# One matmul of 512 columns for the high and low parts of 256 tokens, with the two halves summed at evacuation

## The chip, the cores and the metric

The kernel runs on one core of a Trainium2 chip. The metric is the time of the program on the device in microseconds (us). The core's engines work in parallel, each through its own list of instructions in order, and wait for each other by semaphores: TensorE (PE, matmuls and their weight loads), VectorE (DVE), ScalarE (ACT), GpSimd (POOL), and SyncE (SP), whose queue starts the loads from DRAM.

## The reference

Two layers of a trunk over 256 latent tokens and 256 context tokens of 1024 features. Each layer is FFN 1, a mixing part (attention, spatial gating, short convolution) and FFN 2. What matters here is an FFN:

```python
def ffn_half_step(h, shift, scale, gate, g, w_in, w_out):
    a, b = jnp.split(modulate(rms_norm(h, g), shift, scale) @ w_in, 2, axis=-1)
    return h + FFN_RESIDUAL_WEIGHT * gate * ((jax.nn.silu(a) * b) @ w_out)
```

w_in is 1024 x 5632, w_out 2816 x 1024. The result is the latent stream alone, so the very last FFN (layer 1, FFN 2) works on 256 tokens; the other three work on all 512.

## The kernel before

Everything is feature-major: 128 features on the partitions, tokens along the columns. To keep float32 accuracy, every operand of a product is split into a high and a low part, and a product of two blocks is three matmuls (mm3, lines 383 to 386): high weights with high x, high weights with low x, low weights with high x, all summed in one PSUM bank. x lies in two tiles xh and xl, the gated activations in gh and gl.

The class Weights streams the weights in order of use: SP loads a raw block of 128 x 1024 (at most 6 ahead, RAWB), ScalarE rounds it to the high part whi (line 125), and VectorE or GpSimd subtracts to get the low part wlo (line 126). At most 5 such pairs (SUBB) exist; W.done(i) frees one, and the preparation of the weight five places on is written into the engines' lists at that place. With W.low = "a" the low parts go to VectorE and GpSimd in turn, with "g" all to GpSimd.

The FFN of 256 tokens (function ffn with ntok = 256, so both is False) goes so. first_one does pair 0 of the input blocks feature by feature, while the norm of x is still being finished; its evacuation, and then the preparation of four weights on GpSimd, follow. Then for each pair m = 1 to 21: pair_a multiplies the a block (8 features x 3 matmuls of 256 columns, half_mm), pair_b the b block, and evac forms silu(a) * b and splits it into gh and gl. The order around one pair in the lists of ScalarE and VectorE is: preparation after the a block (its wlo on GpSimd), preparation after the b block (its wlo on VectorE), evacuation. Then 8 output blocks (out_part, three weights each, 22 features of the gated activations x 3 matmuls) and for each of them the residual (resid), which adds to h and sends the block out. Six PSUM banks (mm_bank) turn over. The evacuation is:

```python
            ACT.activation(sa[:, 0:n], ba[:, 0:n], AF.Silu)
            DVE.tensor_tensor(sa[:, 0:n], sa[:, 0:n], bb[:, 0:n], ALU.mult)
            ACT.activation(st["gh"][:, m, 0:n], sa[:, 0:n], AF.Copy)
            DVE.tensor_tensor(st["gl"][:, m, 0:n], sa[:, 0:n], st["gh"][:, m, 0:n].bitcast(F32), ALU.subtract)
```

The order of every engine's list is that in which the code is written; no scheduler moves anything.

Of the kernel before, what the change touches and what calls it, by code (L numbers as in the profile page):

```python
# [39 lines left out]
# packed per-partition parameters: name -> columns for one layer  # L40
# [20 lines left out]
class Weights:  # L61
    """Streams weights in order: DRAM -> raw tile -> (high, low) float32r parts, ahead of their use.
    SPARE in the stream is room of one weight, left to other uses between its take and its done."""
# [29 lines left out]
    def pump(self, preps=None):  # L93
        """Start the loads that have room, and prepare the parts (at most preps, when held back)."""
# [80 lines left out]
def hybrid_trunk_kernel(ctx: ExitStack, tc: tile.TileContext, io: dict, out: bass.AP):  # L175
# [46 lines left out]
    def new_scratch():  # L222
        """4 KB that hold either sums of the adaLN products or the pieces of a norm"""
        t = tp.tile([128, 4, 256], F32, tag="scratch", name="scratch", bufs=1)
        st["scr"], st["scr_u"], st["scr_d"] = t, 0, 0
        return t
# [14 lines left out]
    # ---------------------------------------------------------------- weight specs  # L241
# [16 lines left out]
    # ---------------------------------------------------------------- adaLN  # L258
    pend = []

    def ada_tile(l, c, t):
        """Products of 2 x 128 rows and 512 columns of one chunk, summed over row blocks on VectorE."""
        half, part = divmod(t, 4)

        def fn(W):
            r, raw = W.take_raw()
            if part == 0:
                st["ada"] = new_scratch()
            acc = st["ada"][:, :, :].rearrange("p (s q) n -> p s (q n)", s=2)
            for kk in range(2):  # L270
                k = 2 * part + kk
                src = raw[:, 512 * kk:512 * kk + 512]
                for s in range(2):
                    cv = cs[:, k, s:s + 1]
                    if k == 0:
                        DVE.tensor_scalar(acc[:, s], src, cv, None, ALU.mult)  # L276
                    else:
                        DVE.scalar_tensor_tensor(acc[:, s], src, cv, acc[:, s], ALU.mult, ALU.add)  # L278
            W.done_raw(r)
            if part == 3:  # L280
                a = st["ada"]
                pend.append([2, lambda: ada_sum(l, c, half, a)])
        return fn
# [38 lines left out]
    # ---------------------------------------------------------------- norms over features  # L322
    def stats(acc, sl, n):
        """diagonals of the rstd of each token of sl, from squares summed over blocks in acc."""
        fin = stats_a(acc, sl, n)
        return fin()
# [25 lines left out]
    def split_norm(src, dst_h, dst_l, rb, a, b=None, eng=None):  # L352
        """high and low parts of src * a * rb (+ b); returns the emission of the low part."""
# [9 lines left out]
    st["xh"] = xp.tile([128, DK, NTOK], F32R, name="xh")  # L363
    st["xl"] = xp.tile([128, DK, NTOK], F32R, name="xl")
# [6 lines left out]
    def staggered(makers):  # L371
        """runs emissions that return a follow-up, each follow-up one later"""
# [14 lines left out]

    def mm3x(bank, xh, xl, wh, wl, first, last):
# [4 lines left out]
    # ---------------------------------------------------------------- residual update  # L393
    def resid(l, gc, j, bank, half, first, last_use=False):
        """h += gate * bank, and its squares into the accumulator of the next norm."""
# [4 lines left out]
        if last_use:  # L400
            return
# [11 lines left out]
    # A norm chain for the halves of the stream, cut in steps that are emitted between other work.  # L413
    def chain(l, i, half):
        """generator: each next() emits one step; the steps use PE, ACT and DVE."""
# [17 lines left out]
    # ---------------------------------------------------------------- FFN  # L433
    def ffn(l, which, ntok, tail, first=None):
        """tail(part): called by the last block to start the chain of what follows."""
# [7 lines left out]
        def half_mm(bank, sub, sl):  # L443
            _, wh, wl = sub
            for k in range(DK):
                mm3(bank[:, sl], wh[:, 128 * k:128 * k + 128], wl[:, 128 * k:128 * k + 128],
                    st["xh"][:, k, sl], st["xl"][:, k, sl], k == 0, k == DK - 1)

        def evac(m, ba, bb):
            n = ntok  # L450
            sa = temp(512, "sa", 2)
            ACT.activation(sa[:, 0:n], ba[:, 0:n], AF.Silu)
            DVE.tensor_tensor(sa[:, 0:n], sa[:, 0:n], bb[:, 0:n], ALU.mult)  # L453
# [3 lines left out]
        def start(W):  # L457
            st["gpool"] = ExitStack()
            gp = st["gpool"].enter_context(tc.tile_pool(name=f"g{l}{which}", bufs=1))
            st["gh"] = gp.tile([128, NPAIR, ntok], F32R, name="gh")  # L460
            st["gl"] = gp.tile([128, NPAIR, ntok], F32R, name="gl")
        job(start)

        def first_two(W):
            """Blocks 0 and 1: the latent half while the norm of the context half is under way."""
# [38 lines left out]
        def first_one(W):  # L504
# [6 lines left out]
            for k in range(DK):  # L511
                step(c)
                for bank, (_, wh, wl) in ((ba, a0), (bb, b0)):
                    mm3(bank[:, sl], wh[:, 128 * k:128 * k + 128], wl[:, 128 * k:128 * k + 128],
                        st["xh"][:, k, sl], st["xl"][:, k, sl], k == 0, k == DK - 1)
# [40 lines left out]
        def out_mm(bank, sub, k0, nk, sl, dst=None):  # L556
            _, wh, wl = sub
            dst = sl if dst is None else dst
            for kk in range(nk):
                k = k0 + kk  # L560
                mm3(bank[:, dst], wh[:, 128 * kk:128 * kk + 128], wl[:, 128 * kk:128 * kk + 128],
# [51 lines left out]
    def boundary(l, i):  # L613
        """tail of the last block before norm i of layer l: work(0..2) is the ctx half in three parts."""
# [18 lines left out]
    # ---------------------------------------------------------------- mixing  # L633
    def mixing(l):
# [35 lines left out]
        def tok_part(banks, subs, k0, n, tiles, W=None):  # L670
            """banks[t] += x[:, tile t] of the rows in subs; frees the weights when W is given"""
# [41 lines left out]
        def lat_tr(names, nk, dh, dl, gain):  # L713
            """transposed normalised latents, times their gains, into dh/dl"""
# [16 lines left out]
        # kv latents  # L731
# [49 lines left out]
        def k_prep(W):  # L781
            """shared rope part of the keys: squares, gains, rotation"""
            kpe = P["kpe"]
            # rope tables with the heads' gains
# [66 lines left out]
        # short gated conv, feature-major; blocks c, x, b per 128 channels  # L851
# [38 lines left out]
        # spatial gating: weights loaded whole, transposed by the host  # L890
# [30 lines left out]
        def y_sg(W):  # L921
            """transposed gated features into y blocks 4, 5"""
# [25 lines left out]
        # up-projections, token-major  # L948
# [110 lines left out]
        # attention  # L1059
# [9 lines left out]
        def A(n):  # L1069
            """transposed queries and keys of a head; returns the emissions of the high and the low parts"""  # L1070
# [22 lines left out]
        def B(n, lows):  # L1093
            """scores and their exponentials; lows are emissions of other work, after the maxima"""
# [52 lines left out]
        def C(n):  # L1147
            """transposed probabilities; returns the emissions of their evacuation"""
# [23 lines left out]
        def Dv(j, s, bk):  # L1172
            """probabilities times values of heads 2j and 2j+1, side by side on the array, for one half of the
            queries; returns the emissions of the evacuation and of the squares"""
# [73 lines left out]
        # output projection  # L1248
# [84 lines left out]
    # ---------------------------------------------------------------- program  # L1333
# [50 lines left out]
    def first_blocks(in_spec, evac, half_mm):  # L1384
        """Blocks 0 to 2 of the first FFN: feature by feature, as the modulation of each becomes known."""
# [103 lines left out]
    # order of the weight stream: the adaLN tiles, which wait for their use in place, come a little later  # L1489
# [29 lines left out]
def _layout(i):  # L1519
# [4 lines left out]
    def cols(v):  # L1524
        """[L, n*128] -> [128, L, n]"""
# [3 lines left out]
    def blocks(w, n):  # L1529
        """[L, K*128, N] -> [L, N/n, 128, K, n]"""  # L1530
# [3 lines left out]
    def flat(w):  # L1534
        """[L, K*128, N] -> [L, 128, K*N]"""
# [77 lines left out]
```

## Time and profile before

| | us |
|---|---|
| median of 3 runs | 1778.43 (1777.52 to 1781.66) |
| span of the profiled execution, first to last instruction | 1778.8 |
| TensorE busy in it | 1715.4 (96%) |
| VectorE, ScalarE, GpSimd busy | 1077.7 (61%), 661.1 (37%), 328.9 (18%) |
| mean granted TensorE clock | 0.983 |

The profile gives the span for the profiled execution and no other time of its own. Busy times of TensorE are modelled ends of pipelined matmuls, so rates are read from the distance of starts. A granted clock of 1.00 is 2.4 GHz, 0.50 is 1.2 GHz.

### The profile page before, as it was taken

The page shows a single profiled execution, that of the slowest core. Times are in us where ns is not written, and L with a number is a line of the kernel's source. Part 1 is how long each engine was busy: PE and PEld are TensorE (multiplying, and loading weights), DVE is VectorE, ACT ScalarE, POOL GpSimd, SP SyncE. Part 2 cuts the span into 40 slices and gives each one's busy share as a digit, 9 for nine tenths or more (in the row PEclk, how much of TensorE's full clock was granted, in tenths as well). Part 3 has the DMA queues.
Part 4 walks back from the last instruction along what each step waited for, and adds up shares of the span by engine and source line. Part 5 has one row for each costly group of instructions (what it writes and reads, how often), then busy time and mean ns, then how long its engine had stood idle before and what let it go on. Part 6 is the DMA issues. An engine that isn't in the chain of part 4 may idle for free.

```text
span 1778.8 us, 24162 instructions
## 1 busy us (share of the span) xinstructions
PE 1715.4 (96%) x9422; PEld 1450.0 (82%) x9422; DVE 1077.7 (61%) x1778; ACT 661.1 (37%) x1124; POOL 328.9 (18%) x210
## 2 busy tenths in 40 slices
PE   8999999999998999999999999999999987889999
PEld 6888888889876688888888888888888986589999
DVE  5667777635578475575766356576765577554332
ACT  4422223224457443222232242222222355554442
POOL 0000000004346522000000030000000165465442
PEclk9999999999999999999999999999999998899999
DMA  8545555523211124454555234454454242136553
GB/s 318 189 158 181 184 182 191 178 84 98 82 60 48 37 70 151 134 176 155 165 175 166 98 107 158 162 164 161 158 174 123 70 142 69 36 116 210 185 180 94
DMA packets 71395, 248.59 MB, mean 140 GB/s; under 512 B 8048, under 2 KB 9584, under 8 KB 71280
## 3 DMA queue, kind: packets, MB, share of 16 engines
q1 hardware_dynamic: 71136, 246.97, 42.3%
q8 instruction: 74, 1.21, 0.3%
q14 instruction: 41, 0.34, 0.1%
q10 hardware_dynamic: 144, 0.07, 0.0%
HBM read 245.96 MB, written 1.05 MB: 139 GB/s over the span
## 4 chain that ended last, share of the span: by engine, by line
PE 87%; DVE 7%; ACT 3%; issue 2%; POOL 1%; DMA 1%; ACTq 0%; POOLq 0%; DVEq 0%
PE mm L384 26%; PE mm L385 25%; PE mm L386 25%; PE mm L389 2%; PE mm L391 2%; PE mm L390 2%; PE sm L288 1%; ACT p L1130 1%; PE sm L1181 1%; DVE mx L1119 1%; PE mm L1363 1%; DMA raw<-in_w_ada 1%; DVE xl L361 1%; PE sm L1076 1%; PE mm L1158 1%
## 5 line engine op out<-in xcount | busy, mean ns | idle before, releaser
L384 PE MATMUL mm<-xh,whi 128*128 128x512 f32 (+1 forms) x1712 | 612.0, 358 | 6.5 <-DVE kvl L723 3.1
L385 PE MATMUL mm<-xl,whi 128*128 128x512 f32 (+1 forms) x1712 | 605.7, 354 | 4.0 <-DVE xl L361 3.4
L386 PE MATMUL mm<-xh,wlo 128*128 128x512 f32 (+1 forms) x1712 | 604.1, 353 | 1.8 <-POOL wlo L126 1.3
L125 ACT ACTIVATE whi<-raw 128x1024 fp32r<-128x1024 f32 (+1 forms) x334 | 339.1, 1020 | 486.3 <-PE mm L385 373.6
L126 POOL TENSOR_TENSOR wlo<-raw,whi 128x1024 fp32r<-128x1024 f32 (+3 forms) x112 | 258.1, 2318 | 1335.7 <-ACT whi L125 1320.3
L126 DVE TENSOR_TENSOR wlo<-raw,whi 128x1024 fp32r<-128x1024 f32 (+2 forms) x222 | 265.9, 1199 | 244.8 <-ACT whi L125 244.8
L384 PEld LDWEIGHTS mm<-xh,whi 128*128 128x128 f32 x1712 | 327.4, 191 | 63.9 <-issue 11.8
L385 PEld LDWEIGHTS mm<-xl,whi 128*128 128x128 f32 x1712 | 327.4, 191 | 48.2 <-DVE xl L361 4.5
L386 PEld LDWEIGHTS mm<-xh,wlo 128*128 128x128 f32 x1712 | 327.4, 191 | 45.6 <-POOL wlo L126 1.5
L278 DVE SCALAR_TENSOR_TENSOR scratch<-raw,cs,scratch 128x512 f32<-128x512 f32 x448 | 307.4, 745 | 0.0
L384 PE MATMUL mm<-gh,whi 128*128 128x512 f32 (+1 forms) x770 | 270.2, 351 | 0.0
L386 PE MATMUL mm<-gh,wlo 128*128 128x512 f32 (+1 forms) x770 | 267.1, 347 | 0.0
L385 PE MATMUL mm<-gl,whi 128*128 128x512 f32 (+1 forms) x770 | 267.0, 347 | 0.0
L454 ACT ACTIVATE gh<-sa 128x512 fp32r<-128x512 f32 (+1 forms) x88 | 50.9, 579 | 310.2 <-DVE sa L453 310.2
L384 PEld LDWEIGHTS mm<-gh,whi 128*128 128x128 f32 x770 | 145.8, 189 | 22.3 <-issue 4.9
L386 PEld LDWEIGHTS mm<-gh,wlo 128*128 128x128 f32 x770 | 145.8, 189 | 18.3
L385 PEld LDWEIGHTS mm<-gl,whi 128*128 128x128 f32 x770 | 145.9, 189 | 17.5
L276 DVE TENSOR_SCALAR scratch<-raw,cs 128x512 f32<-128x512 f32 x64 | 28.2, 484 | 148.9 <-PE sm L288 148.9
L455 DVE TENSOR_TENSOR gl<-sa,gh 128x512 fp32r<-128x512 f32 (+1 forms) x88 | 57.7, 656 | 56.8 <-ACT gh L454 56.8
L453 DVE TENSOR_TENSOR sa<-sa,mm 128x512 f32<-128x512 f32 (+1 forms) x88 | 53.9, 613 | 17.7 <-PE mm L386 16.0
L408 DVE TENSOR_TENSOR acc<-acc,sq 128x256 f32<-128x256 f32 x63 | 41.4, 657 | 35.1 <-ACT sq L407 35.1
L360 ACT ACTIVATE xh<-scratch,mods 128x256 fp32r<-128x256 f32 x88 | 42.8, 506 | 52.9 <-DVE scratch L356 52.9
(207 smaller groups left out, 1457.6 us busy)
## 6 DMA issues: line engine op xcount, KB each, us to landing
raw<-in_w_ffn_in SPq DMA_DIRECT2D x176, 512.0 KB, 3.9
raw<-in_w_ada SPq DMA_DIRECT2D x144, 512.0 KB, 4.2
raw<-in_w_ffn_out SPq DMA_DIRECT2D x64, 512.0 KB, 4.4
raw<-in_w_ffn_out SPq DMA_DIRECT2D x32, 384.0 KB, 3.4
raw<-in_w_mo SPq DMA_DIRECT2D x16, 512.0 KB, 3.5
raw<-in_w_cv SPq DMA_DIRECT2D x12, 512.0 KB, 3.7
raw<-in_w_uv SPq DMA_DIRECT2D x8, 512.0 KB, 3.9
raw<-in_w_q SPq DMA_DIRECT2D x8, 384.0 KB, 3.1
```

Source lines behind the costliest of these rows:

```text
L125: nc.scalar.activation(hi[:, a:b], src, AF.Copy)
L126: eng.tensor_tensor(lo[:, a:b], src, hi[:, a:b].bitcast(F32), ALU.subtract)
L278: DVE.scalar_tensor_tensor(acc[:, s], src, cv, acc[:, s], ALU.mult, ALU.add)
L360: ACT.activation(dst_h, u, AF.Identity, bias=b)
L384: PE.matmul(bank, lhsT=wh, rhs=xh, start=first, stop=False)
L385: PE.matmul(bank, lhsT=wh, rhs=xl, start=False, stop=False)
L386: PE.matmul(bank, lhsT=wl, rhs=xh, start=False, stop=last)
L389: PE.matmul(bank, lhsT=xh, rhs=wh, start=first, stop=False)
L408: DVE.tensor_tensor(acc[:, half], acc[:, half], sq, ALU.add)
L453: DVE.tensor_tensor(sa[:, 0:n], sa[:, 0:n], bb[:, 0:n], ALU.mult)
L454: ACT.activation(st["gh"][:, m, 0:n], sa[:, 0:n], AF.Copy)
L455: DVE.tensor_tensor(st["gl"][:, m, 0:n], sa[:, 0:n], st["gh"][:, m, 0:n].bitcast(F32), ALU.subtract)
```

## The change

x2 holds high and low parts of x side by side, [128, 8, 2, 512], and g2 those of the gated activations, [128, 22, 2, tokens]; xh, xl, gh and gl become views of them. In the FFN of 256 tokens mm2 takes the place of mm3: one matmul of 512 columns multiplies the high weights with high and low parts at once, into the two halves of a bank, and one of 256 columns adds low weights times high part to the second half. So an evacuation has to sum the halves: ScalarE copies the first half of each bank to SBUF, VectorE adds the second, and Silu, product and split follow. The residual adds the halves of the output one after the other. The rest of the program keeps its order and its operations. (The lines that only lose comments are left out.)

```diff
+    st["x2"] = xp.tile([128, DK, 2, NTOK], F32R, name="x2")
+    st["xh"] = st["x2"][:, :, 0]
+    st["xl"] = st["x2"][:, :, 1]
...
+    def mm2(bank, wh, wl, x2, first, last):
+        PE.matmul(bank, lhsT=wh, rhs=x2, start=first, stop=False, skip_group_check=True)
+        PE.matmul(bank[:, 256:512], lhsT=wl, rhs=x2[:, 0], start=False, stop=last, skip_group_check=True)
...
         DVE.scalar_tensor_tensor(h[:, j, half], src, mods[:, l, gc, j, s:s + 1], h[:, j, half], ALU.mult, ALU.add)
         if last_use:
+            DVE.scalar_tensor_tensor(h[:, j, half], bank[:, 256:512], mods[:, l, gc, j, s:s + 1], h[:, j, half],
+                                     ALU.mult, ALU.add)
             return
...
             for k in range(DK):
+                if not both:
+                    mm2(bank, wh[:, 128 * k:128 * k + 128], wl[:, 128 * k:128 * k + 128],
+                        st["x2"][:, k, :, sl], k == 0, k == DK - 1)
+                    continue
...
             sa = temp(512, "sa", 2)
-            ACT.activation(sa[:, 0:n], ba[:, 0:n], AF.Silu)
-            DVE.tensor_tensor(sa[:, 0:n], sa[:, 0:n], bb[:, 0:n], ALU.mult)
+            if both:
+                ACT.activation(sa[:, 0:n], ba[:, 0:n], AF.Silu)
+                DVE.tensor_tensor(sa[:, 0:n], sa[:, 0:n], bb[:, 0:n], ALU.mult)
+            else:
+                sb = temp(512, "sa", 2)
+                for part, bk in ((0, ba), (1, bb)):
+                    p = sa[:, 256 * part:256 * part + 256]
+                    ACT.activation(sb[:, 256 * part:256 * part + 256], bk[:, 0:n], AF.Copy)
+                    DVE.tensor_tensor(p, sb[:, 256 * part:256 * part + 256], bk[:, 256:512], ALU.add)
+                ACT.activation(sb[:, 0:n], sa[:, 0:n], AF.Silu)
+                DVE.tensor_tensor(sa[:, 0:n], sb[:, 0:n], sa[:, 256:512], ALU.mult)
             ACT.activation(st["gh"][:, m, 0:n], sa[:, 0:n], AF.Copy)
             DVE.tensor_tensor(st["gl"][:, m, 0:n], sa[:, 0:n], st["gh"][:, m, 0:n].bitcast(F32), ALU.subtract)
...
+            st["g2"] = gp.tile([128, NPAIR, 2, ntok], F32R, name="g2")
+            st["gh"] = st["g2"][:, :, 0]
+            st["gl"] = st["g2"][:, :, 1]
...
                 k = k0 + kk
+                if not both:
+                    mm2(bank, wh[:, 128 * kk:128 * kk + 128], wl[:, 128 * kk:128 * kk + 128],
+                        st["g2"][:, k, :, sl], k == 0, k == NPAIR - 1)
+                    continue
```

first_one calls mm2 in the same way. Two places of the engines' lists show the change. ScalarE, in the input part of this FFN, from the evacuation of one pair to that of the next, before (whi is the high part of a weight, raw the loaded block, mm a PSUM bank, sa the temporary of the evacuation):

```order
L452 ACTIVATE sa<-mm 128x256
L454 ACTIVATE gh<-sa 128x256
L125 ACTIVATE whi<-raw 128x1024 x2
L452 ACTIVATE sa<-mm 128x256
L454 ACTIVATE gh<-sa 128x256
```

The same place with the change (g_12906 is the tile g2):

```order
L473 ACTIVATE sa<-mm 128x256 x2
L475 ACTIVATE sa<-sa 128x256
L477 ACTIVATE g_12906<-sa 128x256
L125 ACTIVATE whi<-raw 128x1024 x2
L473 ACTIVATE sa<-mm 128x256 x2
```

Between the two preparations of one pair and those of the next there are now two copies, Silu and gh in place of Silu and gh. VectorE at the same place, before (wlo is the low part of a weight):

```order
L126 TENSOR_TENSOR wlo<-raw,whi 128x1024
L453 TENSOR_TENSOR sa<-sa,mm 128x256
L455 TENSOR_TENSOR gl<-sa,gh 128x256
L126 TENSOR_TENSOR wlo<-raw,whi 128x1024
L453 TENSOR_TENSOR sa<-sa,mm 128x256
```

And with the change:

```order
L126 TENSOR_TENSOR wlo<-raw,whi 128x1024
L474 TENSOR_TENSOR sa<-sa,mm 128x256 x2
L476 TENSOR_TENSOR sa<-sa 128x256
L478 TENSOR_TENSOR g_12906<-sa,g_12906 128x256
L126 TENSOR_TENSOR wlo<-raw,whi 128x1024
```

Where VectorE had the product alone between its low part and gl, it has two sums with a PSUM operand and then a product of two operands in SBUF.

## Rows read from the trace of the kernel before

**Rows 1.** The page's chain that ended last, share of the span by engine

```profile
PE 87%; DVE 7%; ACT 3%; issue 2%; POOL 1%; DMA 1%; ACTq 0%; POOLq 0%; DVEq 0%
```

**Rows 2.** Window in the last stage: us, busy (instructions) by engine, clock, DMA

```profile
1640.00:1660.00 20.00, 20.00 (x169) 20.00 (x168) 6.37 (x10) 9.18 (x14) 8.76 (x4) 1.00 0.56 192
```

**Rows 3.** Groups by shape, last stage: line, operation, count | busy, mean ns

```profile
L384 PE MATMUL mm<-gh,whi 128*128 128x256 f32 x176 | 49.8, 283 | 0.0
```

**Rows 4.** Timeline of TensorE: 24 starts of 256 columns, 18 of 512

```profile
1649.87 0.28 PE L384 MATMUL mm<-xh,whi 128*128 128x256 f32 x1
...
1652.75 0.28 PE L384 MATMUL mm<-xh,whi 128*128 128x256 f32 x1
...
699.89 0.39 PE L384 MATMUL mm<-xh,whi 128*128 128x512 f32 x1
...
703.97 0.39 PE L384 MATMUL mm<-xh,whi 128*128 128x512 f32 x1
```

**Rows 5.** Timelines of ScalarE, VectorE, GpSimd, one pair [idle before <-releaser]

```profile
1648.56 1.06 ACT L125 ACTIVATE whi<-raw 128x1024 fp32r<-128x1024 f32 x1 [1.71 <-issue]
1649.53 0.37 ACT L452 ACTIVATE sa<-mm 128x256 f32<-128x256 f32 x1
1651.24 0.42 ACT L454 ACTIVATE gh<-sa 128x256 fp32r<-128x256 f32 x1 [1.35 <-DVE sa L453]
1651.57 1.04 ACT L125 ACTIVATE whi<-raw 128x1024 fp32r<-128x1024 f32 x1
1654.32 1.06 ACT L125 ACTIVATE whi<-raw 128x1024 fp32r<-128x1024 f32 x1 [1.71 <-issue]
...
1649.65 1.23 DVE L126 TENSOR_TENSOR wlo<-raw,whi 128x1024 fp32r<-128x1024 f32 x1 [3.30 <-ACT whi L125]
1650.80 0.41 DVE L453 TENSOR_TENSOR sa<-sa,mm 128x256 f32<-128x256 f32 x1
1651.69 0.42 DVE L455 TENSOR_TENSOR gl<-sa,gh 128x256 fp32r<-128x256 f32 x1 [0.48 <-ACT gh L454]
...
1646.92 2.40 POOL L126 TENSOR_TENSOR wlo<-raw,whi 128x1024 fp32r<-128x1024 f32 x1 [3.36 <-ACT whi L125]
```

**Rows 6.** Timeline of GpSimd early in the input part

```profile
1613.22 2.41 POOL L126 TENSOR_TENSOR wlo<-raw,whi 128x1024 fp32r<-128x1024 f32 x1 [2.89 <-ACT whi L125]
1618.52 2.41 POOL L126 TENSOR_TENSOR wlo<-raw,whi 128x1024 fp32r<-128x1024 f32 x1 [2.89 <-ACT whi L125]
```

**Rows 7.** Timelines of GpSimd and VectorE where their operations meet

```profile
1596.13 2.40 POOL L126 TENSOR_TENSOR wlo<-raw,whi 128x1024 fp32r<-128x1024 f32 x1
...
1598.49 3.38 POOL L126 TENSOR_TENSOR wlo<-raw,whi 128x1024 fp32r<-128x1024 f32 x1
...
1597.81 1.80 DVE L126 TENSOR_TENSOR wlo<-raw,whi 128x1024 fp32r<-128x1024 f32 x1 [6.96 <-ACT whi L125]
1599.53 0.41 DVE L453 TENSOR_TENSOR sa<-sa,mm 128x256 f32<-128x256 f32 x1
1600.42 1.73 DVE L455 TENSOR_TENSOR gl<-sa,gh 128x256 fp32r<-128x256 f32 x1 [0.48 <-ACT gh L454]
```

**Rows 8.** Timelines around the first evacuation, and ScalarE at pair 3

```profile
1590.30 4.83 ACT L125 ACTIVATE whi<-raw 128x1024 fp32r<-128x1024 f32 x5
...
1593.85 0.39 PE L386 MATMUL mm<-xh,wlo 128*128 128x256 f32 x1 [1.33 <-POOL wlo L126]
...
1612.10 1.04 ACT L125 ACTIVATE whi<-raw 128x1024 fp32r<-128x1024 f32 x1
```

**Rows 9.** Windows elsewhere in which the granted clock falls

```profile
1024.00:1029.00 5.00, 3.25 (x26) 2.84 (x24) 4.27 (x7) 2.63 (x6) 2.56 (x3) 1.00 0.54 166
1029.00:1033.50 4.50, 4.31 (x23) 4.31 (x24) 4.33 (x10) 1.50 (x4) 2.37 (x1) 0.62 0.31 112
```

**Rows 10.** Timeline at the end: last matmul, last residual

```profile
1775.03 0.28 PE L386 MATMUL mm<-gh,wlo 128*128 128x256 f32 x1
1775.35 0.48 DVE L399 SCALAR_TENSOR_TENSOR h<-mm,mods,h 128x256 f32<-128x256 f32 x1 [7.43 <-PE mm L386]
```

More of the change, by code (lines that the diff above doesn't have):

```diff
@@ L361, in split_norm @@
         return lambda: eng.scalar_tensor_tensor(dst_l, u, b, dst_h.bitcast(F32), ALU.add, ALU.subtract)
-    st["xh"] = xp.tile([128, DK, NTOK], F32R, name="xh")
-    st["xl"] = xp.tile([128, DK, NTOK], F32R, name="xl")
+    st["x2"] = xp.tile([128, DK, 2, NTOK], F32R, name="x2")
+    st["xh"] = st["x2"][:, :, 0]
+    st["xl"] = st["x2"][:, :, 1]
     def mod_chunk(l, i, k, half, rb):
@@ L459, in start @@
             gp = st["gpool"].enter_context(tc.tile_pool(name=f"g{l}{which}", bufs=1))
-            st["gh"] = gp.tile([128, NPAIR, ntok], F32R, name="gh")
-            st["gl"] = gp.tile([128, NPAIR, ntok], F32R, name="gl")
+            st["g2"] = gp.tile([128, NPAIR, 2, ntok], F32R, name="g2")
+            st["gh"] = st["g2"][:, :, 0]
+            st["gl"] = st["g2"][:, :, 1]
         job(start)
@@ L513, in first_one @@
                 for bank, (_, wh, wl) in ((ba, a0), (bb, b0)):
-                    mm3(bank[:, sl], wh[:, 128 * k:128 * k + 128], wl[:, 128 * k:128 * k + 128],
-                        st["xh"][:, k, sl], st["xl"][:, k, sl], k == 0, k == DK - 1)
+                    mm2(bank, wh[:, 128 * k:128 * k + 128], wl[:, 128 * k:128 * k + 128],
+                        st["x2"][:, k, :, sl], k == 0, k == DK - 1)
             finish(c)
```

## Prediction

> **What bounds the kernel now.** I read first the chain of work that ended last: TensorE holds 87% of it [rows 1]. The change touches only the last stage, the second FFN of layer 1, which works on the 256 latent tokens (22 pairs of input blocks, then 8 output blocks). So I read that stage by itself: in a window in its middle TensorE is busy all 20 us at a granted clock of 1.00, the 2.4 GHz level [rows 2]. In the output part alone there are 176 instructions for each of the three products [rows 3]; with 44 × 8 triples of the input part the stage has 352 + 176 = 528 triples.
>
> Next the price of a matmul. 24 starts of 256 columns take 2.88 us, 120.0 ns each; 18 starts of 512 columns take 4.08 us, 226.7 ns each [rows 4]. At 2.4 GHz the columns alone would be 106.7 and 213.3 ns, so either width carries the same 13.3 ns on top.
>
> Then the other engines, because a TensorE that is always busy hides how near they are. One pair is one period: ScalarE's whi starts at 1648.56 and again at 1654.32, so 5.76 us, which is 48 matmuls of 120 ns [rows 5]. Inside it the engines hand each other one chain: GpSimd's wlo (1646.92, 2.40 us, so until 1649.32), VectorE's wlo on the whi of 1648.56 (1649.65), the product of the gate (1650.80), gh on ScalarE (1651.24), then the second whi of the pair (1651.57), on which the next wlo of GpSimd waits; one period after 1646.92 that is 1652.68, 1.11 us behind the whi. Two facts about that chain decide this case.
>
> First, VectorE's wlo starts only 0.33 us after GpSimd's wlo ended [rows 5], and when they meet, one waits for the other. At 1597.81 VectorE's wlo was issued while GpSimd's ran (1596.13 + 2.40 = 1598.53); it took 1.80 us where it takes 1.23 us alone, and ended 1.08 us after GpSimd did. GpSimd's next one, begun at 1598.49, took 3.38 us where 2.40 is its own. gl at 1600.42 took 1.73 us instead of 0.42 and ended at 1602.15, 0.28 us after that GpSimd operation (1601.87). The product L453 at 1599.53, which reads one operand from PSUM, took its 0.41 us beside the same GpSimd operation [rows 5, 7]. So operations with both inputs in SBUF are locked out, those with one in PSUM are not. The Trainium skill, page "SBUF", section "Who interferes with whom", says just this (two SBUF inputs on VectorE contend with a GpSimd instruction that reads SBUF, and the later one fully blocks); the rows agree, and of this change the rule says that a slower evacuation can collide.
>
> Second, where the chain is closed by this lock it has a length of its own: second whi to GpSimd 1.11, GpSimd 2.40, end of VectorE's wlo 1.08 later, then product (starting 0.08 before that end, 0.41), gh (0.03 later), next whi (0.33 later): 5.28 us. The trace shows the chain running so: after the stage's slow start GpSimd's wlos start at 1613.22 and 1618.52, 5.30 us apart [rows 6], catching up on TensorE until its 5.76 us rule again. The slack of this loop is thus 0.46 us a pair.
>
> **The change part by part.**
> TensorE: of each triple the two products with the high weights become one instruction of 512 columns. One start fewer per triple: 226.7 + 120.0 = 346.7 ns instead of 360.0, so 13.3 ns × 528 = 7.0 us over the stage, 16 × 346.7 ns = 5.55 us a pair instead of 5.76. The moving operand now has two pieces of 256, which no row shows; bounds are no cost and 13.3 ns again (nothing gained); I take no cost, since the extra goes by instruction at both widths. The Trainium skill, page "TensorE: Matmul & The Clock Gate", section "Back-to-back issue gap", puts the fixed part at 2.5 ns when warm; by that the stage would gain only 1.3 us. The rows give 13.3 ns at two widths, and I keep those.
>
> Evacuation of a pair: before, Silu from PSUM, product, gh, gl. Now copy a, copy b (ScalarE), sum a, sum b (VectorE), Silu, product, gh, gl. The copies stand behind the first whi and are done while VectorE still works on its wlo, so they cost nothing as long as that wlo covers them (0.7 us for two at 0.37, against 1.23 us or more). After that wlo there was one operation of 0.41 us up to gh. Now there are sum a (0.41, PSUM operand as L453), Silu (from SBUF; between 0.37 as from PSUM and 0.42 as gh; I take 0.42) and the product with both inputs in SBUF (0.42 as gl), with 0.03 us for each of two more handovers: 0.90 us longer. Bounds: 0.82 with the short Silu and one handover less, 1.0 with handovers of 0.06; nothing is excluded, since the three follow from each other. Sum b lies beside Silu.
>
> What that does: the second whi comes 0.9 us later, GpSimd's wlo ends 0.9 us later, and 0.33 us was all the distance that there was to VectorE's wlo. They collide, and the loop closes at 5.30 + 0.90 = 6.20 us a pair. TensorE wants 5.55. Queued behind the blocked wlo are the sums, behind them on ScalarE Silu, gh and both whi: everything that feeds TensorE goes at 6.20. Five prepared weights hide this for some pairs; from then on each pair waits some 0.65 us for a low part.
>
> The sum, in the times of the profiled execution. (1) The first block now waits for the low part of each feature at a still halved clock, and gains a little later: about +0.1. (2) The first evacuation gates five weights: the first whi after it starts at 1590.30, and TensorE goes on at 1593.85, when GpSimd has the low part [rows 8]; the evacuation is 0.9 longer. (3) Three more evacuations until the loop runs free: the second whi of pair 3 stood at 1612.10 [rows 8] and moves by 0.1 + 0.9 + 3 × 0.9, and the product of pair 1 meets a GpSimd operation, which costs about the 1.3 us that gl lost [rows 7]: 5.0 us, so 1617.1. (4) 18 pairs at 6.20: 111.6, so 1728.7 for the place where the next second whi would follow gh of pair 21; its gl ends 0.5 later, 1729.2. (5) TensorE needs that g as block 21 of the first output block and has done all before: it waits there, by about 5 us. From there 1 + 7 × 22 = 155 pairs of matmuls at 346.7 ns: 53.7 us, end near 1783.0. Before, the last matmul started at 1775.03 and its slot ended at 1775.15 [rows 10]: +7.9. (6) The last residual is two operations of 0.48 us, the second waiting for the first: +0.5. (7) A wait of 5 us halves the clock: elsewhere, after 5 us in which TensorE worked 3.25, the next 4.5 us ran at a mean of 0.62 [rows 9], so 3.4 us of them at half, the 1.2 GHz level, which costs up to 1.7; bounds 0 and twice that; I take 1.4. Together +9.8 us. The profiled span of 1778.8 us is 0.4 above the median of 1778.43, so 1788.2 us.
>
> **The rivals.**
> No collision. If VectorE's wlo were not held up (the sum, Silu and product together under 0.33 us, or a blocked wlo that costs nothing), TensorE stays the bound: −7.0, plus 0.9 for the first evacuation, 0.1, 0.5 and 0.3 for triples whose gain falls into waits: −5.2, 1773.2 us. For it speaks that busy shares of ScalarE and VectorE are half empty [rows 2]; against it the 0.33 us and the locked operations in rows 7. Chance 7%.
> Half the length. If the added work took 0.45 us, the loop would be 5.75: 18 × 0.45 = 8.1 us less than in (4), some 1.6 us less in (3), and no wait long enough for (7): −1.3, about 1777 us, no difference. The point where the result turns is about 0.5 us of extra evacuation. Chance 7%.
> No gain per instruction. If the second piece costs 13.3 ns, the loop rules the input part anyway, and the output part loses its 155 × 13.3 ns = 2.1 us: 1790.3 us. Chance 10%, within the slower cases.
>
> **How the numbers follow.** The forecast and its variant with no gain: 86%, slower. Its own range: 18 × ±0.1 us for the loop, ±1.3 for the start, −1.4 to +2 for the clock and 2.1 for the pieces: 1784.5 to 1791.5. For 8 in 10 of all cases I go to 1783.5. A difference of 0.2%, 3.6 us, is about what can be told from none: faster 0.07, same 0.07, slower 0.86.
>
> **What would show it.** After the change: starts of GpSimd's wlo 6.2 us apart in the input part (5.55 would refute the collision); VectorE's wlo near 2.5 us instead of 1.23; from about the middle of the input part on, waits of TensorE for wlo of some 0.65 us once a pair; one wait of about 5 us for gl in the first output block, with a halved clock behind it; matmul starts 226.7 and 120.0 ns apart; two operations of 0.48 us at the end. Wrong would be the forecast if blocked operations overlap after all, or if the preparation runs further ahead than the five weights allow.

## The result, and the profile after

The changed kernel takes 1789.75 us (median of 5 runs, 1788.46 to 1791.44); the kernel before took 1778.43 beside it. The ratio is 1.006, with an interval of 1.0047 to 1.0072: slower by about 11 us. The forecast was 1788.2, and its range of 1783.5 to 1791.5 holds the time.

TensorE's share of the chain that ended last fell; shares of the span by engine, page of the changed kernel:

```profile
PE 79%; DVE 8%; ACT 6%; issue 6%; POOL 1%; DMA 1%; ACTq 0%; POOLq 0%; DVEq 0%
```

It was 87% [rows 1]. What TensorE waits for from 1585 us to the end stands in the view of waits of the changed kernel (engine and line, what it waited for, us in total, times, longest):

```profile
PE mm L394 <- POOL wlo L126: 5.4, 12, 1.9
PE mm L393 <- DVE g L478: 4.5, 1, 4.5
```

Twelve waits are for a low part from GpSimd, and one, of 4.5 us, for the gated activations (g, gl in the kernel before). The first of the twelve, 1.9 us, is the one that the kernel before also had at its first evacuation, there 1.33 us [rows 8]. The loop that makes the other eleven is seen in one pair, in the timelines of ScalarE, VectorE and GpSimd of the changed kernel (start, us, engine, line; in brackets the idle time before and who ended it):

```profile
1588.08 4.83 ACT L125 ACTIVATE whi<-raw 128x1024 fp32r<-128x1024 f32 x5
...
1607.38 1.99 ACT L125 ACTIVATE whi<-raw 128x1024 fp32r<-128x1024 f32 x2
...
1613.57 1.99 ACT L125 ACTIVATE whi<-raw 128x1024 fp32r<-128x1024 f32 x2
...
1644.58 1.99 ACT L125 ACTIVATE whi<-raw 128x1024 fp32r<-128x1024 f32 x2
...
1649.56 0.42 ACT L475 ACTIVATE sa<-sa 128x256 f32<-128x256 f32 x1 [2.44 <-DVE sa L474]
1650.47 0.42 ACT L477 ACTIVATE g<-sa 128x256 fp32r<-128x256 f32 x1 [0.49 <-DVE sa L476]
1650.79 1.99 ACT L125 ACTIVATE whi<-raw 128x1024 fp32r<-128x1024 f32 x2
...
1646.61 2.58 DVE L126 TENSOR_TENSOR wlo<-raw,whi 128x1024 fp32r<-128x1024 f32 x1 [1.47 <-ACT whi L125]
1649.12 0.74 DVE L474 TENSOR_TENSOR sa<-sa,mm 128x256 f32<-128x256 f32 x2
1650.01 0.42 DVE L476 TENSOR_TENSOR sa<-sa 128x256 f32<-128x256 f32 x1 [0.15 <-ACT sa L475]
...
1645.70 2.41 POOL L126 TENSOR_TENSOR wlo<-raw,whi 128x1024 fp32r<-128x1024 f32 x1 [3.80 <-ACT whi L125]
1651.91 2.40 POOL L126 TENSOR_TENSOR wlo<-raw,whi 128x1024 fp32r<-128x1024 f32 x1 [3.80 <-ACT whi L125]
```

Follow it from the whi of 1644.58: GpSimd starts 1.12 us later and runs until 1648.11. VectorE's wlo is issued at 1646.61, while GpSimd runs, and ends at 1649.19, 1.08 us after GpSimd; it takes 2.58 us where it took 1.23 [rows 5]. From its end to the next whi (1650.79) the evacuation takes 1.60 us; before, it was 0.69 us from 1650.88 to 1651.57 [rows 5]. So 1.12 + 2.41 + 1.08 + 1.60 = 6.21 us, which is the distance of the two whi and of GpSimd's two starts, and nothing in this circle waits for TensorE. The hold is what makes the circle long: by an estimate from these rows, a wlo of 1.23 us would have ended at 1647.84, and the circle would be 3.26 + 1.60 = 4.86 us, under the 5.55 that TensorE wants. Two whi now follow each other without a pause (one row x2), where there were 1.71 us of idle time between them [rows 5]. ScalarE stands idle for 2.44 us ahead of its Silu, and the releaser named there, the sum, was itself queued behind the blocked wlo.

What that leaves for TensorE, and the clock behind the long wait, is in the windows of the changed kernel (from:to, us, busy and instructions of PE, PEld, DVE, ACT, POOL, granted clock, DMA share, GB/s):

```profile
1640.00:1660.00 20.00, 19.61 (x112) 16.78 (x110) 13.25 (x16) 10.74 (x21) 8.59 (x4) 1.00 0.50 162
1660.00:1680.00 20.00, 18.87 (x103) 15.45 (x102) 13.66 (x16) 9.83 (x18) 7.69 (x4) 1.00 0.48 159
...
1722.00:1724.00 2.00, 0.00 (x0) 0.00 (x0) 1.94 (x3) 0.35 (x1) 0.20 (x1) 0.88 0.38 61
1724.00:1726.00 2.00, 0.52 (x1) 0.50 (x2) 0.85 (x2) 1.49 (x3) 0.00 (x0) 0.50 0.95 313
1726.00:1728.00 2.00, 2.00 (x8) 1.63 (x6) 0.00 (x0) 1.99 (x4) 0.70 (x1) 0.50 0.39 150
1728.00:1730.00 2.00, 2.00 (x8) 1.71 (x7) 1.80 (x1) 1.11 (x2) 1.94 (x2) 0.50 0.00 0
1730.00:1732.00 2.00, 2.00 (x12) 1.76 (x11) 1.13 (x4) 0.85 (x1) 2.00 (x1) 0.91 0.85 219
```

Around 1650 TensorE is still nearly full, on the weights that were ready; from 1660 on it loses 1.1 us in 20. From 1722 to 1724 no matmul runs, the first after the wait starts at 1725.48, and the granted clock falls to 0.50, the 1.2 GHz level; by the five rows some 6.8 us pass at that level. What a pair of matmuls (512 and 256 columns) takes there is seen in TensorE's timeline of the changed kernel, in which four pairs lie between these two starts:

```profile
1726.29 0.63 PE L393 MATMUL mm<-g,whi 128*128 128x512 f32 x1
...
1728.85 0.63 PE L393 MATMUL mm<-g,whi 128*128 128x512 f32 x1
```

That is 640 ns a pair.

The start and the output part show in TensorE's and VectorE's timelines of the changed kernel:

```profile
1577.81 0.79 PE L393 MATMUL mm<-x,whi 128*128 128x512 f32 x1 [1.64 <-DVE x L361]
...
1585.08 0.39 PE L393 MATMUL mm<-x,whi 128*128 128x512 f32 x1
...
1588.55 0.39 PE L393 MATMUL mm<-x,whi 128*128 128x512 f32 x1
...
1725.48 0.79 PE L393 MATMUL mm<-g,whi 128*128 128x512 f32 x1 [4.51 <-DVE g L478]
...
1744.73 0.40 PE L393 MATMUL mm<-g,whi 128*128 128x512 f32 x1
...
1748.97 0.40 PE L393 MATMUL mm<-g,whi 128*128 128x512 f32 x1
...
1782.18 0.40 PE L393 MATMUL mm<-g,whi 128*128 128x512 f32 x1
...
1782.74 0.48 DVE L407 SCALAR_TENSOR_TENSOR h<-mm,mods,h 128x256 f32<-128x256 f32 x1 [6.77 <-PE mm L394]
1783.26 0.48 DVE L409 SCALAR_TENSOR_TENSOR h<-mm,mods,h 128x256 f32<-128x256 f32 x1
```

From 1585.08 to 1588.55 there are 10 pairs of matmuls, 347 ns each, as forecast; from 1744.73 to 1748.97 there are 12, and they take 353.3 ns each. The last residual stands at 1782.74, and its second half follows at 1783.26, where one operation stood before [rows 10].

**The last FFN by segments.** The stage begins for this count at the load of the Silu table on ScalarE (1578.10 us in the profile before, 1574.13 after) and ends with the last residual. In us:

| segment | before | after | more | forecast |
|---|---|---|---|---|
| table load to TensorE's first matmul | 3.10 | 3.68 | 0.58 | in the next |
| to the first whi behind the first evacuation | 9.10 | 10.27 | 1.17 | 1.0, with the one above |
| to the second whi of pair 3 | 21.80 | 25.49 | 3.69 | 4.0 |
| to the last residual | 163.25 | 169.17 | 5.92 | 4.3 |
| its end | 0.48 | 1.00 | 0.52 | 0.5 |
| sum | 197.73 | 209.61 | 11.88 | 9.8 |

The 11.9 us answer to the 11.3 between the medians. The spans differ by only 7.8 (1786.6 and 1778.8), because the profiled execution before came 4.0 us later to this stage, through parts in which both kernels have the same instructions. So below the stage length of each profiled execution, counted in this way, stands beside the median.

### The profile page after: what moved, and what is told of

Same layout as the page of the kernel before. It is cut to its first block, busy times and chain, and to the rows that moved or that the text cites. A ratio compares the mean times of both kernels' runs of the same rounds, so it can differ in the third digit from the quotient of the medians.

```text
span 1786.6 us, 23263 instructions
## 1 busy us (share of the span) xinstructions
PE 1714.6 (96%) x8894; PEld 1421.1 (80%) x8894; DVE 1123.1 (63%) x1830; ACT 673.3 (38%) x1168; POOL 328.0 (18%) x210
## 4 chain that ended last, share of the span: by engine, by line
PE 79%; DVE 8%; ACT 6%; issue 6%; POOL 1%; DMA 1%; ACTq 0%; POOLq 0%; DVEq 0%
PE mm L386 22%; PE mm L387 22%; PE mm L388 22%; ACT whi L125 3%; PE mm L393 2%; PE mm L399 2%; PE mm L397 2%; PE mm L398 2%; PE mm L394 1%; PE sm L288 1%; ACT p L1158 1%; DVE mx L1147 1%; PE mm L1391 1%; DVE x L361 1%; PE sm L1209 1%
## 5 line engine op out<-in xcount | busy, mean ns | idle before, releaser
L386 PE MATMUL mm<-x,whi 128*128 128x512 f32 (+1 forms) x1360 | 512.0, 376 | 5.5 <-DVE kvl L751 3.1
L387 PE MATMUL mm<-x,whi 128*128 128x512 f32 (+1 forms) x1360 | 505.8, 372 | 4.0 <-DVE x L361 3.4
L388 PE MATMUL mm<-x,wlo 128*128 128x512 f32 (+1 forms) x1360 | 504.3, 371 | 0.5 <-DVE wlo L126 0.5
L386 PEld LDWEIGHTS mm<-x,whi 128*128 128x128 f32 x1360 | 259.5, 191 | 62.2 <-issue 11.8
L387 PEld LDWEIGHTS mm<-x,whi 128*128 128x128 f32 x1360 | 259.6, 191 | 48.6 <-DVE x L361 4.9
L388 PEld LDWEIGHTS mm<-x,wlo 128*128 128x128 f32 x1360 | 259.6, 191 | 44.0 <-DVE wlo L126 0.9
L386 PE MATMUL mm<-g,whi 128*128 128x512 f32 (+1 forms) x594 | 220.4, 371 | 0.0
L388 PE MATMUL mm<-g,wlo 128*128 128x512 f32 (+1 forms) x594 | 217.3, 366 | 0.0
L387 PE MATMUL mm<-g,whi 128*128 128x512 f32 (+1 forms) x594 | 217.2, 366 | 0.0
L386 PEld LDWEIGHTS mm<-g,whi 128*128 128x128 f32 x594 | 112.0, 189 | 22.4 <-issue 4.9
L393 PE MATMUL mm<-x,whi 128*128 128x512 f32 x352 | 127.2, 404 | 1.8 <-DVE x L361 1.6
L388 PEld LDWEIGHTS mm<-g,wlo 128*128 128x128 f32 x594 | 112.0, 189 | 18.4
L387 PEld LDWEIGHTS mm<-g,whi 128*128 128x128 f32 x594 | 112.1, 189 | 17.5
L394 PE MATMUL mm<-x,wlo 128*128 128x256 f32 x352 | 101.1, 287 | 5.1 <-POOL wlo L126 5.1
L393 PEld LDWEIGHTS mm<-x,whi 128*128 128x128 f32 x352 | 67.4, 191 | 18.7 <-DVE x L361 2.4
```

The costliest lines, as they stand in the source:

```text
L386: PE.matmul(bank, lhsT=wh, rhs=xh, start=first, stop=False)
L387: PE.matmul(bank, lhsT=wh, rhs=xl, start=False, stop=False)
L388: PE.matmul(bank, lhsT=wl, rhs=xh, start=False, stop=last)
L393: PE.matmul(bank, lhsT=wh, rhs=x2, start=first, stop=False, skip_group_check=True)
L394: PE.matmul(bank[:, 256:512], lhsT=wl, rhs=x2[:, 0], start=False, stop=last, skip_group_check=True)
```

## The experiments

The theory of the prediction (A in the expectations) is that the longer evacuation closes a loop in which VectorE's low part must wait for GpSimd's. If so, the loop must open when one of its links is taken away, the merged matmul alone must cost nothing, and the evacuation alone must bring the whole loss. The other letters are explained in the expectations where they stand. The kernels ran in two sets, each beside runs of the kernel before, which took 1779.79 in the first (20 runs) and 1779.0 in the second (21 runs).

**1. No low parts on GpSimd from pair 1 on** (set 1). VectorE makes all of them, so it has nobody to wait for; the preparations right behind the first evacuation stay on GpSimd.

```diff
             W.done(b0[0])
-            W.low = "a"
+            W.low = "v"
```

> The changed kernel, but in the last FFN all low parts of weights from pair 1 on are made by VectorE, so GpSimd is out of the loop. Theory A (the loop GpSimd low part, blocked VectorE low part, longer evacuation, next high part paces the input part at 6.20 us a pair): the loop is gone, TensorE paces at 16 times 353 ns = 5.65 us a pair, no wait for gl in the first output block; 11.3 us slower than before turns into about 2 us faster, 1776.5 us. Theory B (the sums and copies themselves, whoever makes the low parts, or the two-piece matmul, hold TensorE back): stays at 1787 to 1791 us. Theory C (VectorE becomes the bound with both low parts): its work in a pair is 2 x 1.23 + 0.74 + 0.42 + 0.42 = 4.0 us, so not expected; it would show VectorE without idle time and more than 1780 us.

1778.58 us (10 runs), ratio to before 0.9989 (0.9978 to 1.0001); stage 197.39 us. Waits, VectorE's timeline and windows of this kernel:

```profile
PE mm L394 <- POOL wlo L126: 1.9, 1, 1.9
```

```profile
1645.39 1.23 DVE L126 TENSOR_TENSOR wlo<-raw,whi 128x1024 fp32r<-128x1024 f32 x1 [0.52 <-ACT whi L125]
```

```profile
1590.00:1592.00 2.00, 2.00 (x9) 1.73 (x8) 1.56 (x1) 0.41 (x1) 2.00 (x2) 0.61 0.71 242
1592.00:1594.00 2.00, 2.00 (x8) 1.69 (x7) 0.49 (x1) 1.00 (x2) 2.00 (x1) 0.54 0.61 205
1640.00:1660.00 20.00, 20.00 (x116) 17.34 (x114) 14.30 (x23) 11.64 (x22) 0.00 (x0) 1.00 0.60 188
```

The evacuation is as long as in the changed kernel, and VectorE has all the low parts to make. Yet its wlo is back at 1.23 us, the wait for g is gone, TensorE is full in the middle, and 11 us of time are back. So it was not the amount of work on VectorE or ScalarE but GpSimd's part in the loop: the hold, or its 2.40 us a low part, which experiment 5 tells apart. Some 2 us under before were expected; the interval doesn't show that this kernel is faster than before. What is left is the wait of 1.9 us at the first evacuation, and in this execution the clock fell behind it as well.

**2. The long evacuation with the old matmuls** (set 1). The kernel before, with copy, VectorE operation with a PSUM operand, Silu and product as in the change; the VectorE operation takes the larger of the copy and the bank, which are the same value.

```diff
...
+                    ACT.activation(sb[:, 256 * part:256 * part + 256], bk[:, 0:n], AF.Copy)
+                    DVE.tensor_tensor(p, sb[:, 256 * part:256 * part + 256], bk[:, 0:n], ALU.max)
+                ACT.activation(sb[:, 0:n], sa[:, 0:n], AF.Silu)
+                DVE.tensor_tensor(sa[:, 0:n], sb[:, 0:n], sa[:, 256:512], ALU.mult)
```

> The kernel before with its three matmuls of 256 columns, but with the evacuation of the last FFN made as long as the changed one: both banks copied to SBUF by ScalarE, VectorE takes the maximum of copy and bank (the same value) where the change adds the halves, then Silu from SBUF and a product of two operands in SBUF. Theory A: the longer evacuation alone closes the loop at 6.20 us a pair although TensorE asks for a pair only every 5.76; some 1790 us, wait of about 4.5 us for gl in the first output block. Theory B' (the matmul of 512 columns in two pieces is what costs): 1778 to 1780 us, starts of GpSimd's low parts 5.76 us apart.

1790.53 us (4 runs), ratio 1.0062 (1.0045 to 1.0079); stage 209.60 us, that of the changed kernel. Waits and GpSimd's timeline of this kernel:

```profile
PE mm L384 <- ACT gh L463: 4.0, 1, 4.0
PE mm L386 <- POOL wlo L126: 3.4, 9, 1.9
```

```profile
1644.54 2.42 POOL L126 TENSOR_TENSOR wlo<-raw,whi 128x1024 fp32r<-128x1024 f32 x1 [3.80 <-ACT whi L125]
1650.76 2.40 POOL L126 TENSOR_TENSOR wlo<-raw,whi 128x1024 fp32r<-128x1024 f32 x1 [3.80 <-ACT whi L125]
```

The same two waits and the same 6.2 us a pair, with not one matmul changed. The evacuation alone costs the whole loss, and the merged matmul gives nothing back that can be told as long as this loop sets the pace.

**3. Edits 1 and 2 together** (set 1): old matmuls, long evacuation, VectorE alone.

> As the run with three matmuls and the long evacuation, but all low parts of the last FFN from pair 1 on on VectorE. Theory A: no collision, TensorE paces at 5.76 us a pair; only the first evacuation is 0.9 us longer: 1779.3 us, no difference that can be told. Theory B (length of the evacuation by itself): as slow as with GpSimd, 1788 to 1791 us.

1780.16 us (10 runs), ratio 1.0007 (0.9996 to 1.0018); stage 199.37 us, and the wait at the first evacuation is the only one from there on. Once its loop is open, the long evacuation costs nothing that the medians can tell; the stage of the profiled execution is 1.6 us longer than before, which is about the first evacuation and the longer wait behind it.

**4. The merged matmul with the old evacuation** (set 1). Silu and product read only the first half of each bank; the sum with the second half is left out.

```diff
...
-                for part, bk in ((0, ba), (1, bb)):
...
+            ACT.activation(sa[:, 0:n], ba[:, 0:n], AF.Silu)
+            DVE.tensor_tensor(sa[:, 0:n], sa[:, 0:n], bb[:, 0:n], ALU.mult)
```

> The changed kernel with the short evacuation of before: Silu and product read the first halves of the banks alone, the second halves (products with low x and low weights) are left out of the input part's result. The matmuls are those of the change, low parts by VectorE and GpSimd in turn. Theory A: the loop stays at 5.3 us, under TensorE's 16 x 353 ns = 5.65 us a pair; the merged matmul alone is worth 528 x 6.7 ns = 3.5 us less 0.5 for the second residual: 1775.5 us. Theory B' (the two-piece matmul costs): 1785 us or more.

1773.46 us (5 runs), ratio 0.9958 (0.9942 to 0.9973): 6.3 us faster, more than was expected. The stage in its profiled execution is 195.38 us, only 2.4 us shorter than before, so for about 4 us of that difference this execution gives no place. GpSimd's timeline of this kernel:

```profile
1642.02 2.41 POOL L126 TENSOR_TENSOR wlo<-raw,whi 128x1024 fp32r<-128x1024 f32 x1 [3.25 <-ACT whi L125]
1647.67 2.41 POOL L126 TENSOR_TENSOR wlo<-raw,whi 128x1024 fp32r<-128x1024 f32 x1 [3.24 <-ACT whi L125]
```

5.65 us a pair are 16 × 353.3 ns: TensorE sets the pace. The loop does not bind: early in the stage, where it catches up, GpSimd's starts are 5.30 us apart here too (1609.18 and 1614.48).

**5. The two engines change places** (set 2). GpSimd makes the low part that stands ahead of the evacuation, VectorE the one behind it; they still take turns.

```diff
-                eng = nc.gpsimd if self.low == "g" or (self.low == "a" and self.prep_i % 2) else nc.vector
+                eng = nc.gpsimd if self.low == "g" or (self.low == "a" and self.prep_i % 2 == 0) else nc.vector
```

> The changed kernel with the two low parts of a pair exchanged: GpSimd makes the one of the weight prepared just ahead of the evacuation, VectorE the one prepared behind it. GpSimd still makes half of them. Theory A (it is the chain second high part, GpSimd, blocked VectorE low part, evacuation that closes): now GpSimd's operation lies beside the copies and sums, which read PSUM and are not held up; only the product waits for its end, some 3.8 us after the first high part starts, the second high part comes at 4.2 and the loop is some 5.2 us, under TensorE's 5.65: no pacing wait, about 1776 to 1779 us. Theory D (any use of GpSimd beside this evacuation holds VectorE up, wherever it lies): 1785 us or more.

1775.07 us (10 runs), ratio 0.9982 (0.9973 to 0.9991); stage 194.08 us. Timelines of GpSimd and VectorE of this kernel:

```profile
1642.14 2.40 POOL L126 TENSOR_TENSOR wlo<-raw,whi 128x1024 fp32r<-128x1024 f32 x1 [3.14 <-ACT whi L125]
1647.69 2.42 POOL L126 TENSOR_TENSOR wlo<-raw,whi 128x1024 fp32r<-128x1024 f32 x1 [3.15 <-ACT whi L125]
...
1642.37 0.75 DVE L474 TENSOR_TENSOR sa<-sa,mm 128x256 f32<-128x256 f32 x2 [0.42 <-ACT sa L473]
1643.28 1.55 DVE L476 TENSOR_TENSOR sa<-sa 128x256 f32<-128x256 f32 x1 [0.16 <-ACT sa L475]
...
1646.26 1.23 DVE L126 TENSOR_TENSOR wlo<-raw,whi 128x1024 fp32r<-128x1024 f32 x1 [0.52 <-ACT whi L125]
```

Here the evacuation itself meets GpSimd (1642.14 to 1644.54). Both sums, with a PSUM operand, go through beside it in 0.75 us; the product, with two operands in SBUF, takes 1.55 us instead of 0.42 and ends at 1644.83, 0.29 us after GpSimd. The Trainium skill, page "SBUF — State Buffer", section "Who interferes with whom", draws the line just there: a VectorE instruction with at most one SBUF input does not contend with GpSimd, one with two SBUF inputs contends with a GpSimd instruction that reads SBUF. The rows agree. One lock a pair is paid, 1.1 us, and still the pace is 5.55 us a pair, TensorE's. So here a lock costs time only where it closes a loop longer than TensorE's period: GpSimd's work now stands beside the sums and not ahead of them. What the expectation calls D has fallen, and so has GpSimd's 2.40 us by themselves as the cause of the loss, since they are still paid once a pair. The median lies 1 us under the range that was expected, with pairs of matmuls at 5.55 / 16 = 0.347 us, where 0.353 had been put.

**6. Edit 1, and the first preparations ahead of the first evacuation** (set 2). In first_one the preparation of two weights, on VectorE, is written ahead of the evacuation that it stood behind.

```diff
             W.hold = False
+            W.low = "v"
+            W.pump(2)
             evac(0, ba, bb)
             W.done(a0[0])
             W.done(b0[0])
-            W.low = "a"
```

> The changed kernel with the low parts of the last FFN on VectorE, and with two weights prepared ahead of the first evacuation instead of behind it. Theory A: besides the loop the wait of 1.9 us behind the first pair is gone too, and with it a halved clock that follows it in some executions; against the run with VectorE alone 2 to 3.5 us less, some 4.5 us below before: 1774.5 us. If that wait was hidden or moves to the next weight: as the run with VectorE alone.

1770.36 us (5 runs), ratio 0.9959 (0.9945 to 0.9972): faster than both kernels, and 4 us under what was expected. The stage takes 189.86 us, and TensorE has no wait in it from 1585 us on. Window and TensorE's timeline of this kernel:

```profile
1640.00:1660.00 20.00, 20.00 (x117) 17.48 (x116) 13.96 (x21) 12.49 (x21) 0.00 (x0) 1.00 0.60 193
```

```profile
1699.88 0.39 PE L393 MATMUL mm<-x,whi 128*128 128x512 f32 x1
...
1705.08 0.40 PE L393 MATMUL mm<-g,whi 128*128 128x512 f32 x1
```

15 pairs in 5.20 us, 346.7 ns each, without a seam from the input part (x) to the output part (g). Against kernel 1 the stage is 7.5 us shorter. 1.9 us are the wait; about 1.7 us the clock (some 3.4 us at half); and some 500 pairs at 346.7 ns instead of the 353.3 that kernel 1 shows are 3.3 us: 6.9 us together.

**7. The kernel before with the two edits of 6** (set 2).

> The kernel before, with its three matmuls and short evacuation, and with the same two edits (low parts on VectorE, two weights prepared ahead of the first evacuation). It tells what of the gain of the other run is the merged matmul's. Its wait behind the first pair was 1.5 us: 1.5 us less than before, 1777.5 us; the merged matmul is then worth the rest, 528 x 6.7 ns = 3.5 us less 0.5 for the second residual. If the merged matmul is worth nothing, both runs are equal.

1778.39 us (11 runs), ratio 0.9997 (0.9987 to 1.0007); stage 196.22 us, no wait either from 1585 us on. The edits alone bring the old kernel nothing that the medians can tell (its wait behind the first pair, which the expectation gives as 1.5 us, was 1.33 [rows 8], and the stage is 1.5 us shorter). What the merged matmul is worth, once nothing else binds, is the distance between 6 and 7: 8.0 us by the medians, 6.4 by the stages, more than twice what the expectation gave it with 6.7 ns a pair; the prediction's 13.3 ns × 528 are 7.0.

**8. The low product into the first half** (set 2), to see whether writing the second half a second time makes the 353.3 ns.

```diff
-        PE.matmul(bank[:, 256:512], lhsT=wl, rhs=x2[:, 0], start=False, stop=last, skip_group_check=True)
+        PE.matmul(bank[:, 0:256], lhsT=wl, rhs=x2[:, 0], start=False, stop=last, skip_group_check=True)
```

> The changed kernel, but the product with the low weights is added to the first half of the bank instead of the second (the sum of the halves is the same). It looks at the 353.3 ns of a pair of matmuls where 346.7 were expected. If it is the writing of the second half by two instructions in a row that costs, a pair takes 346.7 ns; if not, a mean of 353.3 again. The time stays at some 1789 us, since the loop of 6.20 us a pair paces.

1789.73 us (1 run), stage 210.70 us; the 4.5 us wait for g is there, and TensorE's pairs go in the same two rhythms, 347 and 353.3 ns. By this one run it is not the half that is written.

## Why the prediction was right

**The bound and the price of a matmul.** The bound was right, the price in part. Kernels 5 and 6 show 346.7 ns over whole stretches, so the two pieces of the moving operand need cost nothing. But the rhythm is not always that: where nothing holds it, the changed kernel mostly goes at 353.3 ns, and of the forecast gain of 13.3 ns half is left. The Trainium skill, page "TensorE: Matmul & The Clock Gate", section "Back-to-back issue gap", has a formula for an isolated matmul, columns at 2.4 GHz and 2.5 ns on top; an estimate from it is 325 ns for the two. No stretch here shows that.

**The evacuation, 0.90 us longer.** Measured 0.91: 1.60 against 0.69 us from the end of VectorE's wlo to the next whi.

**The collision and the loop at 6.20 us.** Right in each link, and shown, not only argued: 1 and 5 take the lock out of the loop in two ways and the time falls below or to that of before, 2 makes the loop with the old matmuls, 3 opens it again, 4 has the merged matmul without the loop. With it the rival of no collision falls; what it describes, TensorE as the bound, is seen in 4 to 6, where something else had to be changed. Half the length falls with the 0.91. No gain per instruction falls with the 346.7 and with the 6.4 us between 6 and 7; in the output part of the changed kernel half of it came true.

**Steps (1) and (2), 1.0 us.** Measured 1.75. The evacuation part is right; step (1) was mis-sized. TensorE's first matmul now needs the low part of x on VectorE (line 361, 1.64 us of waiting in the row of 1577.81) where it needed the high part on ScalarE; that alone is 0.58 us, and the block from there to its evacuation is another 0.27 longer; 0.1 was taken for the whole step. The gain that was set against it is not to be had at the low clock. At 0.50 a pair of matmuls takes 640 ns, which is its 768 columns at 1.2 GHz with nothing on top, and so did the three matmuls before; TensorE's timeline of the kernel before, in its first block at a granted clock of 0.50:

```profile
1582.32 0.41 PE L384 MATMUL mm<-xh,whi 128*128 128x256 f32 x1
...
1582.96 0.41 PE L384 MATMUL mm<-xh,whi 128*128 128x256 f32 x1
```

**Step (3), 4.0 us beyond them.** Measured 3.7, but that it comes so near is in part luck. The sum let each of three evacuations come 0.9 us later. In the traces GpSimd works through a row of low parts behind the first evacuation without a pause, first in the kernel before, then in the changed one:

```profile
1591.42 18.91 POOL L126 TENSOR_TENSOR wlo<-raw,whi 128x1024 fp32r<-128x1024 f32 x7 [16.79 <-ACT whi L125]
...
1589.20 15.50 POOL L126 TENSOR_TENSOR wlo<-raw,whi 128x1024 fp32r<-128x1024 f32 x6 [20.10 <-ACT whi L125]
```

VectorE's wlo is held to 1.08 us behind the end of that row, and the evacuation follows: before, 1610.33 + 1.08 + 0.69 is the second whi of pair 3, at 1612.10; after, 1604.70 + 1.08 + 1.60 is that of pair 2, at 1607.38, and one turn of the loop, 6.19 us, leads to pair 3 at 1613.57. So the lock ruled this stretch in both kernels.

**Step (4).** From the second whi of pair 3 (1613.57) to TensorE's going on with g (1725.48) 111.9 us, forecast 112.1.

**The waits of each pair.** Forecast 0.65 us from the middle of the input part on. They begin there (the first after 1650), and a pair loses 6.20 − 16 × 0.3533 = 0.55 us. The view of waits shows less, (5.4 − 1.9) / 11 = 0.32 us, since part of that time passes while the matmul ahead still runs in the record; by the starts, the pair of matmuls with the second of these waits takes 0.90 us (1659.89 to 1660.79), 0.55 more than its neighbours.

**Steps (5) to (7).** The wait for g is 4.5 us where about 5 was forecast. From its end to the last residual it takes 57.26 us, forecast 55.4 with the clock. The 155th pair would start at 1725.48 + 154 × 0.3533 = 1779.89 and starts at 1782.18: 2.3 us for the clock, where 1.4 was taken, inside the bounds of 0 to 3.4. Too short was the stretch at the low level, 3.4 us from rows 9: here it is some 6.8, of which TensorE works from 1725.48 on, some 4.9 us at 640 ns a pair. The other 1.0 us is 154 × 6.6 ns of the slower rhythm. The second residual is 0.52.

So the sum is 9.8 forecast and 11.9 measured: 0.7 for the start of the first block, 0.9 for the clock, 1.0 for the rhythm, −0.5 for (3) and (4). The last step, from the span of the profiled execution to the median of whole runs, compares unlike things, since a run is some 1.85 us longer than its span (after: 1788.46 and 1786.6). It does no harm: to take 0.4 us off that span is the same as to add the 9.8 to the median of 1778.43.

## What to carry to other kernels

An engine that is always busy hides how near the loop behind it is: before adding work to an evacuation, close the circle of the other engines (here ScalarE, GpSimd, VectorE and back) and compare its length with the period of the bound; with 0.46 us of slack, 0.91 us of added work turned a gain of 6 to 8 us into a loss of 11. Where two engines lock each other out, it matters which operation meets which: put the one engine's long operation beside the other's operations with a PSUM operand, or take it off that engine. And measure a new instruction with the loop open, else an experiment shows the loop and says nothing about the instruction.

## What the runs showed of the hardware that was not expected

The same stream, one matmul of 512 columns and one of 256 with new weights each, goes in more than one steady rhythm: 347 ns a pair in the changed kernel from 1585.08 on and in kernels 5 and 6, 353.3 ns in the changed kernel from 1744.73 on and, throughout the middle of the stage, in kernels 1 and 4, at a granted clock of 1.00 each time. In the changed kernel it went over from one to the other across the wait of 1591.61, and back without any wait in the view, in TensorE's timeline of the changed kernel:

```profile
1644.47 0.40 PE L393 MATMUL mm<-x,whi 128*128 128x512 f32 x1
...
1647.65 0.40 PE L393 MATMUL mm<-x,whi 128*128 128x512 f32 x1
...
1648.74 0.39 PE L393 MATMUL mm<-x,whi 128*128 128x512 f32 x1
...
1651.86 0.39 PE L393 MATMUL mm<-x,whi 128*128 128x512 f32 x1
```

Nine pairs lie between the first two starts, 353.3 ns each, and nine between the last two, 346.7 ns each. Kernel 8, in its one run, speaks against the half of the bank that is written as the reason. What sets the rhythm is open; it is worth up to 528 × 6.6 ns = 3.5 us here.
